# Sample tile last, the first FFN product's operands in the gate's room, weight sums in two sets of tiles: a hybrid S5 and attention layer on one core

## The chip, the cores and the metric

The kernel runs on one core of a Trainium2 chip. Its time is what the device takes for one execution, in microseconds (us); lower is better. A core has five engines with instruction streams of their own: TensorE (PE, matrix products, with a weight load PEld before each), VectorE (DVE), ScalarE (ACT), GpSimd (POOL) and SyncE (SP), which here issues all DMA transfers. An engine works through its stream in order; between engines, semaphores say when an operand is ready.

## What is computed

One layer over 2048 prompt frames and 32 sample frames of width 1024, all in float32. Cut to what matters here:

```python
h = rmsnorm(x, ln1_g) * (1 + sc1) + sh1                 # sc, sh, g1, g2 from c @ w_ada
q, k, v, u = split(h @ w_in)                            # 8 heads, 2 kv heads, 512 state space columns
attn = window_attention(rope(norm(q)), rope(norm(k)), v)   # own chunk of 64 and 128 frames before
y, state = s5(u)                                        # per 16 channels a 64-dim complex scan
g = gelu(y);  ssm_o = g * sigmoid(g @ ssm_glu_w + ssm_glu_b)
x = x + g1 * (concat(rmsnorm(attn), rmsnorm(ssm_o)) @ w_out)
h2 = rmsnorm(x, ln2_g) * (1 + sc2) + sh2
y = x + g2 * ((silu(h2 @ w_gate) * (h2 @ w_up)) @ w_down)   # D_FF = 2816
```

The sample frames take the same layer with a key cache and a state that is handed in. The kernel also returns the last keys, values and states.

## The kernel before

**Precision.** Each float32 operand of a large product is split into a rounded high part and the rest (`split`: a copy on ACT, a subtraction on DVE), and `mm3` makes three matmuls of it: high by high, high by low, low by high.

**Tiles and stages.** The prompt is 16 tiles of 128 frames, the sample is a 17th (number `NPT` = 16) of 32 frames. Stage A makes the projections; stage B runs the state space groups (`ssm_group`, 32 of them) beside attention; stage C (from about 556 to 1011 us) forms the gate of the state space group and the output projection; then comes the FFN.

**Order in stage C.** `TILES` lists the tiles in the order in which attention and the output work on them: the sample, then 8 to 15, then 0 to 7 (tiles 0 to 5 are projected late). `UNITS` lists the gate's units, a unit being two tiles: 8 (the sample alone), then 4 to 7, 0 to 3. Four generators are stepped in turn by the `while` loop at line 1537, through the class `Flow`, one live item each (attention: two):

- `fa`, `attention_tile`: at most `NATT` = 6 tiles ahead of the finished outputs. A softmax goes from TensorE (`s`) over DVE, ACT (`pbuf`) and POOL (`pbuf`) back to TensorE (`pt`, `ob`).
- `fp`, `c_prep` (line 1285): one gate unit. `g_load` brings the gelu of the state space output in (`gr`; for the sample through the DRAM tensor `gs_d` and a transpose of `gn`), `gh` and `gl` are its parts, products with `glh` and `gll` go to the banks `cb`, a tanh makes `z`, and `mh`, `ml` are the gated value's parts. Its limit is `fc.done() // 2 + 2`.
- `fq`, `c_norm` (line 1332): loads the residual `xc`, splits the attention tile into `ah`, `al` and forms both scales (`rb`, `rso`).
- `fc`, `c_out` (line 1363): 48 matmuls of 512 columns (32 for the sample) in two halves to the banks `co`, the scales, the adaLN gate `g1b` on POOL, the residual, and a store to `x1_d`. It is stepped `CST` = 2 times a round. The sample's operand holds high and low part side by side, and `fold` adds the two row groups.

The text order of the program is not the order on the engines: the tile framework's planner (`schedule_with_timeline_sim=True`) lays each engine's stream out at build time from the order of the text and simulated times, and may move what it holds ready ahead.

**Into the FFN.** When attention is through, `ffn_open` and `h_steps(0)` transform the first six finished prompt tiles into the FFN's input quadrants (`q`, from transposes in `ft`). The FFN (three blocks of frames, each a gate-and-up layer `i = 0` and three down layers) makes each 2 by 2 block product with seven products instead of eight (`PRODUCTS`); `steps` numbers them, seven per unit. `start_unit` loads the weight quarters of a unit (`wr`) and forms two sums on POOL; `prepare(n)` forms step n's left operand (`wh`, `wl`), three steps ahead; `prepare_right(n)` forms the right one (`bh`, `bl`, from the quadrants `q`). Both write tiles of the pool `pv`, which is opened after `cin.close()` has closed all pools of stage C.

**Weight sums.** During the first layer of the first block, `down_sums` forms the sums of the down weights that all three blocks read: 12 groups, for each four quarters loaded into the tiles `acc0` to `acc3`, four additions on POOL (a fifth tile, `acc4`, takes one result `ds`), each followed at once by a store to `sd_d`. It is advanced by one step in each product and by two in every fourth.

Of the kernel before, what the change touches and what calls it, by code (L numbers as in the profile page):

```python
# [51 lines left out]
TILES = [NPT, *range(8, NPT), *range(8)]  # L52
UNITS = [8, 4, 5, 6, 7, 0, 1, 2, 3]
# [20 lines left out]
def hybrid_kernel(  # L74
# [1022 lines left out]
    def attention_tile(j):  # L1097
# [21 lines left out]
        if j < NPT:  # L1119
            vcur = kv_split(kf, vf, kt[:, :, 128:256], n)  # L1120
            if j == 8:
# [134 lines left out]

    def cbank(shape, dt=F32, nm="cb"):
        return cs1.tile(shape, dt, tag="cb", name=nm, bufs=CB)
# [11 lines left out]
    def g_load(b):  # L1270

        g = pc2.tile([128, 4, LC, 64], F32, tag="gr", name="gr", bufs=1)
# [12 lines left out]
    def c_prep(u):  # L1285
# [13 lines left out]
        gh = pc2.tile([128, 4, 256], F32R, tag="gh", name="gh", bufs=1)  # L1299
        gl = pc2.tile([128, 4, 256], F32R, tag="gl", name="gl", bufs=1)  # L1300
# [25 lines left out]
        if u in (8, 5, 7, 1):  # L1326
            g_load({8: 2, 5: 3, 7: 0, 1: 1}[u])
# [35 lines left out]
    def c_out(j):  # L1363
# [13 lines left out]
        for h in range(2):  # L1377
# [28 lines left out]
    fp_ = {}  # L1406

# [106 lines left out]
    def down_sums():  # L1514

        for L in layers[1:4]:
            for u in range(2):
                for m in range(2):
                    r = {t: quarter(L, u, m, t, pv.tile([128, 2 * HW], F32, tag=f"acc{i}", name="dq")[
                        :, 0:L.kt * 128].rearrange("p (k n) -> p k n", n=128)) for i, t in enumerate(WHERE)}  # L1520
                    s1 = pv.tile([128, 2 * HW], F32, tag="acc4", name="ds")[:, 0:L.kt * 128].rearrange(
                        "p (k n) -> p k n", n=128)
                    yield 1
                    for i, (o, x, y, op) in enumerate(((s1, r["21"], r["22"], ADD), (r["21"], r["11"], r["21"], SUB),
                                                       (r["11"], s1, r["11"], SUB), (r["12"], r["12"], r["11"], SUB))):
                        tt(P, o, x, y, op)
                        SP.dma_start(sd_d[(L.i - 1) * 4 + 2 * u + m, (0, 2, 1, 3)[i], :, 0:L.kt * 128],
                                     o.rearrange("p k n -> p (k n)"))
                        yield 1

    cg = wo_steps(range(4, 8), stage, 512)
    fp = Flow(c_prep, 9, 1, 0)
    fq = Flow(c_norm, NT, 1, 0)
    fc = Flow(c_out, NT, 1, 0)
    wn = 0
    hg = [None]
    while True:
        more = fa.step(fc.done() + NATT)
        fp.step(fc.done() // 2 + 2)
        for _ in range(CWS):  # L1540
            wn += 1
            advance(cg)
        fq.step(min(fa.done(), 2 * fp.done() - 1, fc.done() + 2))
        if wn > WN:
            for _ in range(CST):
                more = fc.step(fq.done()) or more
        if fa.next == fa.n and not fa.live:
            if hg[0] is None:
                ffn_open()
                hg[0] = h_steps(0)  # L1550
            elif fc.done() >= 7:
                if (layers[0], 0) not in raw:
                    start_unit(0)
                advance(hg[0])
        if not more:
            break
    if hg[0] is None:
        ffn_open()
        hg[0] = h_steps(0)
    for _ in hg[0]:  # L1560
        pass
    if "x1" in dbg:
        SP.dma_start(dbg["x1"], x1_d)
    cin.close()
    ptop.close()
    if upto == "C":
        return
# [235 lines left out]
```

## Time and profile before

| | us |
|---|---|
| median of 3 runs (2440.96 to 2443.54) | 2442.73 |
| profiled execution, its own time | 2443.45 |
| its span, first to last instruction | 2441.7 |
| TensorE busy in the span | 2236.6 |
| VectorE busy | 1771.0 |
| ScalarE busy | 1259.8 |
| GpSimd busy | 1341.2 |
| last output matmul of stage C ends | 1010.9 |
| first FFN matmul starts | 1017.04 |

The mean granted clock of TensorE over the span is 0.954 of full speed. How to read the views that follow: a row of *stretches* gives the length of a part of the span, then for each engine its busy time there and the number of its instructions, then the clock that was granted to TensorE in it, the share of the DMA engines' time and the rate. A row of *waits* gives who waited, for whom, the total, how often, the longest. A row of the *timeline* gives start, length, engine, line, operation, output and inputs; in brackets the idle time of that engine before it and what ended it. Most lines are those of helpers (L89 is `tt`, L101 `act`, L117 `mm`), so the tile names tell the instructions apart. `SPq` is SP issuing a transfer.

### The profile page before, as it was taken

Reading aid. Unit: us, or ns where it says so; the run is one execution under the profiler, and the core shown is the slowest. Engines: PE = TensorE matmul, PEld = TensorE weight load, DVE = VectorE, ACT = ScalarE, POOL = GpSimd, SP = SyncE. Lnnn points to the kernel's source line nnn. Section 1 sums busy time; section 2 is a strip of 40 time slices with the busy share of each in tenths; the row PEclk is TensorE's granted clock in tenths of the full one; section 3 lists DMA queues with packets and bytes.
Section 4 is the critical chain, followed back from the end, with each engine's and each line's share of the span. In section 5 each row is a group of like instructions: output and inputs, shape, how many; then the busy total and the mean of one; then the engine's idle time right before and its main releaser. Section 6 shows DMA issues by size and latency. Waiting matters only on the chain.

```text
span 2441.7 us, 39053 instructions
## 1 busy us (share of the span) xinstructions
PE 2236.6 (92%) x13262; PEld 2071.0 (85%) x13262; DVE 1771.0 (73%) x2722; ACT 1259.8 (52%) x2547; POOL 1341.2 (55%) x1205
## 2 busy tenths in 40 slices
PE   7888897987987889789999999999999989999998
PEld 4677676776777777689899998999999989999998
DVE  6979865787666654576666888865578887777787
ACT  6655433556555555433444557444456664444664
POOL 1277866782644545688855235655542366565232
PEclk7899998997998898889999999999999999999999
DMA  7757767754222124368743654543346446433653
GB/s 232 263 178 212 224 205 229 240 181 142 68 65 72 48 59 149 118 194 255 213 124 105 185 161 153 184 139 119 101 131 205 136 121 183 144 109 99 201 156 124
DMA packets 429573, 380.13 MB, mean 156 GB/s; under 512 B 57326, under 2 KB 358986, under 8 KB 429372
## 3 DMA queue, kind: packets, MB, share of 16 engines
q1 hardware_dynamic: 429372, 377.63, 50.6%
q8 instruction: 104, 1.70, 0.3%
q14 instruction: 97, 0.79, 0.1%
HBM read 284.63 MB, written 92.91 MB: 155 GB/s over the span
## 4 chain that ended last, share of the span: by engine, by line
PE 47%; DVE 4%; DMA 2%; issue 1%; POOL 1%; ACT 0%; SPq 0%; DVEq 0%; POOLq 0%; ACTq 0%
PE fx L117 27%; PE fy L117 13%; PE fz L117 6%; DVE wl L89 2%; DVE bl L89 1%; DMA wr<-in_w_up_dram 1%; POOL dq L89 1%; DMA dq<-in_w_down_dram 1%; PE fo L1640 0%; DVE q L89 0%; POOL c L89 0%; DMA xf<-x_d 0%; PE ft L1437 0%; POOL wr L89 0%; DVE xr L89 0%
## 5 line engine op out<-in xcount | busy, mean ns | idle before, releaser
L89 DVE TENSOR_TENSOR wl<-wr,wh 128x512 fp32r<-128x512 f32 (+1 forms) x714 | 722.9, 1030 | 241.8 <-ACT wh L101 237.7
L101 ACT ACTIVATE wh<-wr 128x512 fp32r<-128x512 f32 (+1 forms) x714 | 434.1, 616 | 561.5 <-PE fx L117 303.2
L117 PE MATMUL fx<-bh,wh 128*128 128x352 f32 (+1 forms) x1584 | 514.3, 325 | 18.5 <-ACT c L101 8.3
L117 PE MATMUL fx<-bh,wl 128*128 128x352 f32 (+1 forms) x1584 | 513.8, 324 | 5.4 <-DVE wl L89 5.4
L117 PE MATMUL fx<-bl,wh 128*128 128x352 f32 (+1 forms) x1584 | 512.9, 324 | 6.1 <-DVE bl L89 6.1
L89 POOL TENSOR_TENSOR wr<-wr 128x512 f32<-128x512 f32 x264 | 394.3, 1503 | 162.2 <-DVE wl L89 145.3
L117 PEld LDWEIGHTS fx<-bh,wh 128*128 128x128 f32 x1584 | 302.3, 191 | 21.4 <-ACT c L101 9.3
L117 PEld LDWEIGHTS fx<-bl,wh 128*128 128x128 f32 x1584 | 302.9, 191 | 7.1 <-DVE bl L89 7.0
L117 PEld LDWEIGHTS fx<-bh,wl 128*128 128x128 f32 x1584 | 301.8, 191 | 6.1 <-DVE wl L89 6.0
L117 PE MATMUL fy<-bh,wl 128*128 128x352 f32 (+1 forms) x792 | 255.9, 323 | 8.2 <-DVE wl L89 8.2
L117 PE MATMUL fy<-bh,wh 128*128 128x352 f32 (+1 forms) x792 | 255.3, 322 | 2.2 <-DVE acc L98 2.2
L117 PE MATMUL fy<-bl,wh 128*128 128x352 f32 (+1 forms) x792 | 254.8, 322 | 0.0
L89 POOL TENSOR_TENSOR c<-c 128x352 f32<-128x352 f32 (+1 forms) x99 | 146.5, 1481 | 166.2 <-ACT wh L101 107.6
L89 POOL TENSOR_TENSOR c<-c,acc 128x352 f32<-128x352 f32 (+1 forms) x72 | 84.3, 1175 | 173.2 <-ACT c L101 169.7
L117 PEld LDWEIGHTS fy<-bh,wl 128*128 128x128 f32 x792 | 149.9, 189 | 8.7 <-DVE wl L89 8.7
L89 POOL TENSOR_TENSOR q<-q,q 128x1408 f32<-128x1408 f32 (+3 forms) x24 | 87.8, 3661 | 118.9 <-DVE q L89 86.7
L89 DVE TENSOR_TENSOR bl<-q,bh 128x1408 fp32r<-128x1408 f32 (+3 forms) x84 | 148.8, 1773 | 5.6 <-ACT bh L101 5.6
L117 PEld LDWEIGHTS fy<-bh,wh 128*128 128x128 f32 x792 | 150.4, 190 | 2.7 <-DVE acc L98 2.7
L117 PEld LDWEIGHTS fy<-bl,wh 128*128 128x128 f32 x792 | 150.3, 190 | 0.0
L101 ACT ACTIVATE bh<-q 128x1408 fp32r<-128x1408 f32 (+3 forms) x84 | 107.7, 1284 | 51.5 <-DVE q L89 28.2
L117 PE MATMUL fz<-bh,wl 128*128 128x352 f32 (+1 forms) x396 | 129.5, 327 | 2.3 <-DVE wl L89 2.2
L117 PE MATMUL fz<-bh,wh 128*128 128x352 f32 (+1 forms) x396 | 128.6, 325 | 3.1 <-ACT wh L101 3.0
(386 smaller groups left out, 5214.9 us busy)
## 6 DMA issues: line engine op xcount, KB each, us to landing
wr<-in_w_gate_dram SPq DMA_DIRECT2D x132, 256.0 KB
wr<-in_w_up_dram SPq DMA_DIRECT2D x132, 256.0 KB
wr<-sd_d SPq DMA_DIRECT2D x96, 256.0 KB
wr<-in_w_down_dram SPq DMA_DIRECT2D x72, 256.0 KB
adw<-in_w_ada_dram SPq DMA_DIRECT2D x64, 256.0 KB
f_d<-c SPq DMA_DIRECT2D x88, 176.0 KB
sm<-sm_d SPq DMA_DIRECT2D x32, 448.0 KB
q<-f_d SPq DMA_DIRECT2D x16, 704.0 KB
```

The source lines that it names most:

```text
L89: e.tensor_tensor(out, a, b, op=op)
L101: A.activation(out, a, func, **kw)
L117: PE.matmul(out, lhsT, rhs, start=start, stop=stop, skip_group_check=more)
```

## The change

The sample goes to the end of both lists, and what followed from its first place is adapted (which prompt unit loads the next `gr`, the limit of `c_norm`, the row at which the earlier keys are loaded). The gate's working tiles get a pool of their own, `pcg`, opened last; once the last gate unit is through, `left_open` closes it and opens the pool `pfv` in its room, which holds the left operands of each fourth step and the right operand `b11` of the first product. `prepare(0)` is called right then, inside the loop. `h_steps(0)` is advanced by two steps a round and from six finished tiles on. `down_sums` works in place in two sets of four tiles, loads a group while the one before is added, and issues each store two additions later; it is advanced by one step in each product, and what is left of it is run at the start of the first down layer.

```diff
-TILES = [NPT, *range(8, NPT), *range(8)]
-UNITS = [8, 4, 5, 6, 7, 0, 1, 2, 3]
+TILES = [*range(8, NPT), *range(8), NPT]
+UNITS = [4, 5, 6, 7, 0, 1, 2, 3, 8]
...
+    pcg_ = ExitStack()
+    pcg = pcg_.enter_context(tc.tile_pool(name="pcg", bufs=1, reuse_waits="tile"))
...
-        g = pc2.tile([128, 4, LC, 64], F32, tag="gr", name="gr", bufs=1)
+        g = pcg.tile([128, 4, LC, 64], F32, tag="gr", name="gr")
...
-        gh = pc2.tile([128, 4, 256], F32R, tag="gh", name="gh", bufs=1)
-        gl = pc2.tile([128, 4, 256], F32R, tag="gl", name="gl", bufs=1)
+        gh = pcg.tile([128, 4, 256], F32R, tag="gh", name="gh")
+        gl = pcg.tile([128, 4, 256], F32R, tag="gl", name="gl")
...
-            z = pc2.tile([128, 2, 256], F32, tag="z", name="z")
+            z = pcg.tile([128, 2, 256], F32, tag="z", name="z", bufs=2)
...
-        if u in (8, 5, 7, 1):
-            g_load({8: 2, 5: 3, 7: 0, 1: 1}[u])
+        if h:
+            g_load({2: 3, 3: 0, 0: 1, 1: 4}[b])
...
-                ta, to = (pc2.tile([128, 512], F32, tag="z", name="fo")[0:n] for _ in range(2))
+                fo = pc2.tile([128, 4, 256], F32, tag="sq", name="fo", bufs=1)[0:n].rearrange("p (a k) n -> p a (k n)", a=2)
+                ta, to = fo[:, 0], fo[:, 1]
...
+    def left_open():
+
+        pcg_.close()
+        fp_["v"] = ctx.enter_context(tc.tile_pool(name="pfv", bufs=1, reuse_waits="tile", side="right"))
...
-            h, l = (pv.tile([128, 4, 128], F32R, tag="wv", name=nm, bufs=4 * AHEAD + 4)[:, 0:L.kt] for nm in ("wh", "wl"))
+            h, l = ((pv if n % 4 else fp_["v"]).tile([128, 4, 128], F32R, tag="wv", name=nm, bufs=12 if n % 4 else 4)[
+                :, 0:L.kt] for nm in ("wh", "wl"))
...
-            h, l = (pv.tile([128, 4, HW], F32R, tag=f"b{t}{bn}", name=f"b{t}")[:, 0:L.kt, 0:w] for t in "hl")
+            h, l = ((fp_["v"] if i == 0 else pv).tile([128, 4, HW], F32R, tag=f"b{t}{bn}", name=f"b{t}")[
+                :, 0:L.kt, 0:w] for t in "hl")
...
+    def down_sums():
+
+        groups = [(L, u, m) for L in layers[1:4] for u in range(2) for m in range(2)]
+        got = {}
+
+        def load(i):
+            if i < len(groups):
+                L, u, m = groups[i]
+                got[i] = {t: quarter(L, u, m, t, pv.tile([128, 2 * HW], F32, tag=f"acc{4 * (i % 2) + k}", name="dq")[
+                    :, 0:L.kt * 128].rearrange("p (k n) -> p k n", n=128)) for k, t in enumerate(WHERE)}
+
+        def store(o):
+            L, u, m, s, x = o
+            SP.dma_start(sd_d[(L.i - 1) * 4 + 2 * u + m, s, :, 0:L.kt * 128], x.rearrange("p k n -> p (k n)"))
+
+        load(0)
+        out = []
+        for i, (L, u, m) in enumerate(groups):
+            yield 1
+            r = got.pop(i)
+            for s, o, x, y, op in ((0, "22", "21", "22", ADD), (2, "21", "11", "21", SUB), (1, "11", "22", "11", SUB),
+                                   (3, "12", "12", "11", SUB)):
+                tt(P, r[o], r[x], r[y], op)
+                out.append((L, u, m, s, r[o]))
+                if len(out) > 2:
+                    store(out.pop(0))
+                if s == 2:
+                    load(i + 1)
+                yield 1
+        for o in out:
+            store(o)
...
-        fq.step(min(fa.done(), 2 * fp.done() - 1, fc.done() + 2))
+        fq.step(min(fa.done(), 2 * fp.done(), fc.done() + 2))
...
-            elif fc.done() >= 7:
+            elif fc.done() >= 6:
                 if (layers[0], 0) not in raw:
                     start_unit(0)
-                advance(hg[0])
+                advance(hg[0], 2)
+                if fp.next == fp.n and not fp.live and "v" not in fp_:
+                    left_open()
+                    prepare(0)
...
     for n in range(6):
-        prepare_right(n)
-        if n < AHEAD:
+        if (layers[0], n) not in right:
+            prepare_right(n)
+        if n < AHEAD and n not in left:
             prepare(n)
...
         if li == 0 and u:
-            advance(sums, 1 + (n % 4 == 0))
+            advance(sums)
+        elif li == 1 and (u, p) == (0, 0):
+            for _ in sums:
+                pass
```

More of the change, by code (lines that the diff above doesn't have):

```diff
@@ L1120, in attention_tile @@
             vcur = kv_split(kf, vf, kt[:, :, 128:256], n)
-            if j == 8:
+            if j == TILES[0]:
                 pkv = pb2.tile([128, 2, 128], F32, tag="ckv", name="pkv", bufs=1)
@@ L1512, in load_left @@
                 raw[n, m] = x
[L1514 to L1542, printed above, removed]
-        fq.step(min(fa.done(), 2 * fp.done() - 1, fc.done() + 2))
[L1544 to L1550, printed above, removed]
-            elif fc.done() >= 7:
-                if (layers[0], 0) not in raw:
-                    start_unit(0)
-                advance(hg[0])
-        if not more:
-            break
@@ L1557, in hybrid_kernel @@
[L1557 to L1567, printed above, removed]
-    pv = ctx.enter_context(tc.tile_pool(name="pv", bufs=1, reuse_waits="tile"))
-    pwr = ctx.enter_context(tc.tile_pool(name="pwr", bufs=1, reuse_waits="tile", side="right"))
-    fs1 = ctx.enter_context(tc.tile_pool(name="fs1", bufs=1, space=bass.MemoryType.PSUM, reuse_waits="tile", side="right"))
@@ new lines, in hybrid_kernel @@
+    cg = wo_steps(range(4, 8), stage, 512)
+    fp = Flow(c_prep, 9, 1, 0)
+    fq = Flow(c_norm, NT, 1, 0)
+    fc = Flow(c_out, NT, 1, 0)
+    wn = 0
+    hg = [None]
+    while True:
+        more = fa.step(fc.done() + NATT)
+        fp.step(fc.done() // 2 + 2)
+        for _ in range(CWS):
+            wn += 1
+            advance(cg)
+        fq.step(min(fa.done(), 2 * fp.done(), fc.done() + 2))
+        if wn > WN:
+            for _ in range(CST):
+                more = fc.step(fq.done()) or more
+        if fa.next == fa.n and not fa.live:
+            if hg[0] is None:
+                ffn_open()
+                hg[0] = h_steps(0)
+            elif fc.done() >= 6:
+                if (layers[0], 0) not in raw:
+                    start_unit(0)
+                advance(hg[0], 2)
+                if fp.next == fp.n and not fp.live and "v" not in fp_:
+                    left_open()
+                    prepare(0)
+        if not more:
+            break
@@ new lines, in hybrid_kernel @@
+    if hg[0] is None:
+        ffn_open()
+        hg[0] = h_steps(0)
+    for _ in hg[0]:
+        pass
+    if "v" not in fp_:
+        left_open()
+    if "x1" in dbg:
+        SP.dma_start(dbg["x1"], x1_d)
+    cin.close()
+    ptop.close()
+    if upto == "C":
+        return
+    pv = ctx.enter_context(tc.tile_pool(name="pv", bufs=1, reuse_waits="tile"))
+    pwr = ctx.enter_context(tc.tile_pool(name="pwr", bufs=1, reuse_waits="tile", side="right"))
+    fs1 = ctx.enter_context(tc.tile_pool(name="fs1", bufs=1, space=bass.MemoryType.PSUM, reuse_waits="tile", side="right"))
@@ L1728, in hybrid_kernel @@
         if li == 0 and u:
[L1729 removed]
+            advance(sums)
+        elif li == 1 and (u, p) == (0, 0):
+            for _ in sums:
+                pass
         load_left(n + FAR)
```

## The prediction

> **What bounds the kernel now.** I read the page, then the busy time by stretches of the span, then TensorE's waits where it is not busy, and last the rows around the stage borders.
>
> ```profile
> PE   7888897987987889789999999999999989999998
> ...
> PEclk7899998997998898889999999999999999999999
> ```
>
> From the middle on, the FFN, TensorE is full at full clock; the first half is not. The change touches the second part of that half, the output stage (from 556 us), and the head of the FFN (1011 to 1221 us). By stretches (columns: length, busy time and instructions of PE, weight loads, DVE, ACT, POOL, then granted clock, DMA share, GB/s):
>
> ```profile
> 556.00:620.00 64.00, 46.28 (x265) 39.02 (x265) 50.60 (x96) 40.09 (x99) 17.14 (x16) 0.79 0.40 119
> 620.00:1011.00 391.00, 339.80 (x1962) 296.18 (x1960) 221.85 (x390) 196.18 (x516) 204.27 (x188) 0.91 0.25 80
> 1011.00:1060.00 49.00, 25.00 (x90) 22.73 (x91) 44.41 (x28) 20.88 (x29) 41.00 (x21) 0.69 0.50 151
> 1060.00:1127.00 67.00, 67.00 (x418) 66.91 (x417) 45.61 (x48) 27.89 (x55) 59.66 (x41) 1.00 0.77 238
> 1127.00:1221.00 94.00, 84.50 (x506) 82.33 (x505) 58.58 (x65) 37.62 (x76) 82.36 (x61) 0.98 0.73 222
> 1221.00:1330.00 109.00, 109.00 (x682) 109.00 (x681) 71.10 (x89) 50.89 (x99) 64.83 (x47) 1.00 0.37 110
> ```
>
> TensorE is the engine that the others must feed in every row but one: in 1011 to 1060 DVE is busy 44.41 of 49. The last row gives TensorE's pace, 109.00/682 = 0.160 us a matmul. By it the 90 matmuls of 1011 to 1060 are 14.4 us of work, so **34.6 us** are lost there, and in 1127 to 1221 506 matmuls are 81.0 us, so **13** are lost. In the output stage 64 - 46.28 = 17.7 us and 391 - 339.80 = 51.2 us are idle, beside time at a lower clock. TensorE's longest wait in the steady part (from 620; total, times, longest):
>
> ```profile
> PE pt L1069 <- POOL pbuf L89: 25.5, 5, 8.2
> ```
>
> and at the start (556 to 620):
>
> ```profile
> PE cb L1281 <- DMA gn<-gs_d: 7.1, 1, 7.1
> ```
>
> Half of the steady idle time is waits on a softmax. The long ones come at a rhythm. The busy time of the instructions on the output banks `co` alone, in three stretches:
>
> ```profile
> 692.00:727.00 35.00, 21.33 (x84) 14.75 (x82) 2.24 (x3) 2.03 (x3) 1.00 0.21 72
> 678.00:688.00 10.00, 0.00 (x0) 0.00 (x0) 0.58 (x1) 0.72 (x1) 0.68 0.20 51
> 735.00:745.00 10.00, 0.00 (x0) 0.00 (x0) 0.66 (x1) 0.69 (x1) 0.56 0.00 0
> ```
>
> and of all instructions, in two:
>
> ```profile
> 692.00:727.00 35.00, 34.81 (x222) 30.62 (x220) 20.08 (x37) 18.25 (x52) 16.72 (x17) 1.00 0.21 72
> 678.00:692.00 14.00, 6.07 (x23) 5.21 (x22) 10.67 (x20) 7.35 (x26) 8.38 (x8) 0.63 0.14 37
> ```
>
> Where output matmuls run, TensorE has no gap (34.81 of 35), attention's chains included. Where none runs, at 678 and again at 735, it idles and then runs at half clock. So the stage has a hole in its supply of output matmuls every other tile.
>
> **The change, part by part.** The sum is made against the profiled execution's 2443.45 us (its span is 2441.7; the median of the runs shown, 2442.73, is 0.7 less).
>
> *A, start of the output stage.* The sample tile leaves the front. With it go the round trip through `gs_d` (7.1 us, above) and the need for the gate's prompt operands to come second; its matmuls move to the end. In their place the first prompt unit's load is now what starts the stage:
>
> ```profile
> 588.12 3.03 SPq L1275 DMA_DIRECT2D gr<-gt_d  x4
> 592.85 1.11 ACT L101 ACTIVATE gh<-gr 128x512 fp32r<-128x512 f32 x1 [4.47 <-DMA gr<-gt_d]
> ```
>
> Today it is issued at 588, and ACT has it 4.7 us later. Moved to about 558 it stands on SP's queue before the `w_out` loads and behind the last `gt_d` store, and its 4.7 us lie beside the attention tiles that are in flight, where today's 7.1 did not since the transposes of `gn` stood before those tiles in TensorE's order. I take a gain of 7. From below, the load could hold up SP and the first gate for twice its 4.7 us (-9); from above, all of the 17.7 us idle could go and the loss by the clock (at 0.79 some 27 of the 64 us are at half, at least 9 of them busy, so 5 to 13 lost): 31. Attention's first six tiles are worked ahead of this stage, and one of them is now a prompt tile in place of the sample: the same matmuls, moved to a stretch where the page has 7 to 9 tenths; I cost it at nothing, since what it adds there it saves here.
>
> *B, steady part.* This term comes from the loop, not from an edited instruction. A gate unit takes eight rounds (seven yields), a `c_norm` four, a `c_out` five (nine yields, two calls a round). Unit u may start at `fc.done() >= 2u-2`. Today position 0 is the sample, so unit u holds positions 2u-1 and 2u, and 2u-2 done means that the *first* tile of unit u-1 has just ended. Seven rounds of gate and three of norm follow before the next output can start, and the second tile of unit u-1 covers five: 15 rounds for two tiles, five without output. That is the hole seen above. After the change unit u holds positions 2u and 2u+1, and the same condition means that unit u-2 has ended; the ten rounds of gate and norm lie exactly beside the ten of unit u-1's two outputs. `2*fp.done()` in place of `2*fp.done()-1` says the same. So the hole closes, with the same matmuls.
>
> Its price comes from the hole at 678: 14 - 6.07 = 7.9 us idle; at 0.63 some 10.4 of the 14 us are at half clock, 2.4 to 6.1 of them busy, which loses 1.2 to 3 more. So about 10 a hole. Seven pairs of tiles (391 us at some 55) follow one another here, and the last two have no attention left to wait for; five such holes make 50; the waits themselves are covered rather than gone, and where the planner's guess of a softmax is short TensorE will still stand, so I keep a quarter back and take **38**. Bounds: 0, if the holes stay, and 65, all of 51.2 and 2 us of clock for each of seven pairs. DVE (222 of 391 busy) and ACT (196) have room for a shorter stage. `h_steps`, which forms the FFN's input, must still be through by its end, in 40 rounds fewer:
>
> ```profile
> L101 ACT ACTIVATE q<-ft,sh,sc x24: 368/615/697, 938.8 to 982.9; 128x352 f32<-128x352 f32 x8, 128x32 f32<-128x32 f32 x8, 128x320 f32<-128x320 f32 x8
> ```
>
> Today it ends 28 us ahead of the last output (about 1011). It now goes two steps a round, 11 rounds for its 22, from six finished tiles on: the output matmuls still cover it, at nothing; uncovered its 24 evictions would be 15 us.
>
> *C, border to the FFN.* The timeline of the border, for ACT, SP's queue and TensorE:
>
> ```profile
> 1014.48 0.63 ACT L101 ACTIVATE t<-xc 128x512 f32<-128x512 f32 x1 [4.75 <-POOL xc L89]
> 1015.02 0.19 ACT L101 ACTIVATION_READ_ACCUMULATOR t<-xc 128x1 f32 x1
> 1015.11 1.36 ACT L101 ACTIVATE bh<-q 128x1408 fp32r<-128x1408 f32 x1
> ```
>
> ```profile
> 1014.89 2.14 SPq L1482 DMA_DIRECT2D dq<-in_w_down_dram  x4
> ```
>
> ```profile
> 1017.04 0.66 PE L117 MATMUL fx<-bh,wh 128*128 128x352 f32 x1 [6.13 <-ACT wh L101]
> ```
>
> Nothing that writes the FFN pool `pv` is issued on an engine before that engine's last instruction of the output stage: ACT had been idle for 4.75 us, its operand `q` was complete (row above), and still `bh` follows `t<-xc`. I read this as the planner's order at the pool's opening. The change frees the room of the gate's working tiles early (`pcg`) and puts the first product's weights and `b11` there, so ACT's three splits, DVE's `bl`, two `wl` and `b12 - b11`, and POOL's `b22 - b12` and four `wr` differences no longer stand behind the border. What such instructions cost there (groups by form, 1011 to 1060; busy us, mean ns), and `wl` later on (1221 to 1330):
>
> ```profile
> L89 DVE TENSOR_TENSOR wl<-wr,wh 128x512 fp32r<-128x512 f32 x15 | 22.2, 1518 | 0.0
> L89 DVE TENSOR_TENSOR bl<-q,bh 128x1408 fp32r<-128x1408 f32 x7 | 18.5, 2658 | 1.1 <-ACT bh L101 1.1
> L89 DVE TENSOR_TENSOR q<-q,q 128x1408 f32<-128x1408 f32 x2 | 4.3, 2162 | 0.0
> ```
>
> ```profile
> L89 POOL TENSOR_TENSOR wr<-wr 128x512 f32<-128x512 f32 x8 | 18.2, 2284 | 4.4 <-DVE wl L89 4.4
> ```
>
> ```profile
> L89 DVE TENSOR_TENSOR wl<-wr,wh 128x512 fp32r<-128x512 f32 x58 | 58.8, 1024 | 26.3 <-ACT wh L101 26.2
> ```
>
> DVE, without a gap here, sets the first unit's pace. It loses 2.66 + 2.16 + 2 x 1.52 = **7.9 us** of work. Nothing else is taken from the chain: the second product still waits for the border, and it then becomes what is late, 24 matmuls or 3.8 us after the first. The sample tile as the last one lengthens the tail before the border:
>
> ```profile
> L128 DVE COPY fo<-co x4: 682/682/682, 600.7 to 615.5; 32x512 f32<-32x512 f32 x4
> L89 DVE TENSOR_TENSOR fo<-fo,co x4: 669/676/676, 602.5 to 618.7; 32x512 f32<-32x512 f32 x4
> ```
>
> ```profile
> 607.70 1.70 POOL L89 TENSOR_TENSOR t<-t,g1b 32x512 f32<-32x512 f32 x1 [0.75 <-DVE t L98]
> ```
>
> One fold stands behind its last matmul, 0.68 + 0.68, and a 32-row step of POOL is no shorter than a whole one; I charge the fold and half such a step, 2.2. New on SP's queue is the reload of `g1b` for 32 rows, which waits for POOL's last use by tile 7; behind it stand tile 7's stores, and nothing on TensorE's path reads those. Last, `wl` takes 1518 ns here against 1024 later, where POOL does less: 13 us of POOL work gone (four `wr`, one `q`) may give back half of that difference over the 13 `wl` left, 3.2. Sum 7.9 - 2.2 + 3.2 = **9**; bounds -3 (only the longer tail) and 22.
> The Trainium skill, SBUF — State Buffer, section "SBUF: two separate sides", says that a DVE instruction with two SBUF inputs and a GpSimd instruction exclude each other and that the loser blocks for the other's whole length. By that rule the 13 us moved would free DVE for up to 13 us and C would be 19, unless the weight sums fill the place at once, when it would be 6. The two `wl` rows agree in sign, at 0.5 us on an average `wl` and not a whole POOL instruction, so 19 (a time of 2371) stays an end of the range; the 6 is R4 below.
>
> *D, weight sums.* The additions on POOL (shortest, median, longest ns):
>
> ```profile
> L89 POOL TENSOR_TENSOR dq<-dq x24: 992/1462/1750, 1028.5 to 1209.4; 128x512 f32<-128x512 f32 x16, 128x384 f32<-128x384 f32 x8
> L89 POOL TENSOR_TENSOR ds<-dq x12: 1007/1468/2660, 1021.4 to 1202.6; 128x512 f32<-128x512 f32 x8, 128x384 f32<-128x384 f32 x4
> ```
>
> POOL's other work from 1014 to 1215:
>
> ```profile
> L89 POOL TENSOR_TENSOR wr<-wr 128x512 f32<-128x512 f32 x47 | 76.8, 1648 | 4.4 <-DVE wl L89 4.4
> ```
>
> ```profile
> L89 POOL TENSOR_TENSOR c<-c 128x352 f32<-128x352 f32 x16 | 21.0, 1311 | 0.0
> ```
>
> and who waited from 1000 to 1215, on SP's queue, POOL and ACT:
>
> ```profile
> SPq L1482 <- DMA sd_d<-dq: 17.7, 12, 4.8
> ```
>
> ```profile
> POOL dq L89 <- DMA dq<-in_w_down_dram: 11.5, 4, 6.8
> ```
>
> ```profile
> ACT wh L101 <- POOL wr L89: 28.2, 9, 9.4
> ACT wh L101 <- DMA wr<-in_w_up_dram: 23.6, 8, 6.3
> ```
>
> A unit of seven products is 168 x 0.160 = 27 us of TensorE. POOL owes it 8 `wr` (13.2) and 3 `c` (3.9), 17.1 us. Of 60 sum steps 48 are additions of about 1.47. At 5 steps in 4 products (today) a unit adds 7 of them, 10.3, and POOL needs 27.4 of 27, with its waits more: it is late, `wr` is late, ACT waits for it. At one step a product (after) it adds 5.6, 8.2, and needs 25.3. The same instructions end later, at step 67 of 77. The fifth tile goes, the second set of four lets a group load while the other is added (11.5 us of POOL's waiting), and a store is issued two additions after its own, so that SP less often stands for POOL. Still, a load into a set must wait for that set's stores, and the last of these is issued just ahead of it, so the 17.7 us of SP waiting, with `wr` loads behind, stay in part. Of the 13 us I take **8**; bounds -2 and 13.
>
> **Sum**: 7 + 38 + 9 + 8 = 62; 2443.45 - 62 = 2381.
>
> **The rivals.**
> *R1, the holes stay.* The order of the engines is the planner's and not the loop's; it has shown that it moves work ahead (SP loads `dq` at 1014.89 for a step that is written seven products later). Then B is 0 to 10, and the time about 2443.45 - (7 + 5 + 9 + 8) = 2414. For it: the waits at the holes are attention chains that exist in either order. Against: a planner can only fill with what is ready, and no output is.
> *R2, attention starves (slower).* Output matmuls now always stand between attention's. A tile's chain crosses TensorE some ten times (`qb` twice, `kb`, `s` twice, `pt` three or four times, `ob` twice), and each time 12 output matmuls may stand in front (84 of them take 21.33 us, so 3 us): up to 30 us a tile, 15 with two in flight, 165 over the 11 tiles left. A quarter of that, 41, with B gone and 24 from the rest, is 17 slower: 2460. It decides from 24/11 = 2.2 us a tile on. Against it: 692 to 727 holds both kinds, with no gap.
> *R3, the operands are not early.* `prepare(0)` is called in the loop, `prepare_right(0)` only behind it; if the planner leaves `bh` and `bl` behind the border, C is -2.2 + 3 = 1 and the time 2389.
> *R4, the sums fill the first unit.* With two sets loaded, up to eight additions are ready there in place of today's six; if DVE then gets nothing back, C is 5.7, and if `wr` is late as before, D is 0: 2393.
>
> **How the numbers follow.** Forecast (about 2350 to 2405) 0.55, R1 0.20, R3 0.08, R4 0.07, R2 0.06, and 0.04 that A to D net to nothing. The low end, 2350, is A to D at 15 + 55 + 14 + 10 = 94 saved; the high end, 2424, at 0 + 8 + 5 + 6 = 19, R1 with less from the rest. They leave out R2, the case of nothing and some of the forecast's and R1's edges, two in ten. A measurement of this kernel can tell about 0.2% (4.9 us) from no change: faster 0.55 + 0.20 + 0.08 + 0.07 = 0.90, the same 0.04, slower 0.06.
>
> **What would show it.** A: no `gn` wait near 560, the first 12-matmul group on prompt operands before 600. B: no stretch of 10 us without `co` between the second tile and the last, granted clock near 1.0, the stage some 45 us shorter. C: `fx` within 1 us of the last `co`, a stall at the second product. D: 1.0 clock and no `wr` waits where 1127 to 1221 was. Wrong would make it: the `pt` waits still at a pair's rhythm (R1), `rb` or `al` waiting for attention (R2), `bh` still behind the last `t<-xc` (R3).

## The result, and the profile after

| | before | after |
|---|---|---|
| median, 4 runs each, side by side | 2443.14 (2440.96 to 2448.02) | 2380.72 (2379.13 to 2381.01) |
| ratio, with its 95% interval | | 0.9741 (0.9724 to 0.9757) |
| profiled execution, its span | 2443.45, 2441.7 | 2380.64, 2378.8 |
| mean granted clock | 0.954 | 0.962 |

The time fell by 62.4 us. The page's slices, after (the same two rows as before):

```profile
PE   7898998997999999699999998999999989999998
...
PEclk8898998999899999799999999999999999999999
```

The output stage is slices 10 to 17 in both: 7 9 8 7 8 8 9 7 became 7 9 9 9 9 9 9 6, and the 6 is the border to the FFN. By stretches, after (columns as before; the first row is the whole output stage, the others its parts and the head of the FFN):

```profile
559.00:963.00 404.00, 365.30 (x2172) 315.98 (x2173) 288.05 (x469) 229.52 (x594) 237.43 (x208) 0.93 0.31 97
559.00:620.00 61.00, 47.50 (x261) 39.62 (x262) 49.88 (x80) 40.02 (x90) 24.53 (x18) 0.80 0.48 151
620.00:963.00 343.00, 317.80 (x1912) 276.36 (x1912) 238.16 (x389) 189.50 (x505) 212.89 (x190) 0.95 0.28 88
963.00:1008.00 45.00, 29.48 (x139) 27.54 (x138) 42.00 (x29) 21.57 (x34) 37.14 (x21) 0.80 0.67 201
1008.00:1070.00 62.00, 61.73 (x376) 61.15 (x374) 47.71 (x44) 25.07 (x50) 62.00 (x42) 0.97 0.90 274
1070.00:1159.00 89.00, 83.17 (x497) 82.54 (x498) 66.25 (x67) 38.13 (x76) 81.80 (x59) 0.96 0.68 208
```

The steady part lost 48 us of length (391 to 343). Of the 51.2 us that TensorE stood idle in it, 25.2 are left, and its busy time fell by 22 us with 50 matmuls fewer in the stretch (8 us at its pace), the rest going with the granted clock (0.91 to 0.95). From the stage's end on TensorE does 139 matmuls in 45 us, against 90 in 49 before. TensorE's longest waits in the steady part, after:

```profile
PE pt L1069 <- POOL pbuf L89: 10.8, 4, 5.3
PE co L117 <- DVE fo L89: 3.7, 1, 3.7
PE pt L1069 <- DVE st L89: 3.7, 1, 3.7
```

The wait on a softmax is 10.8 us where it was 25.5. The second row is new: it lies in the sample tile's tail.

To place every gain, the span of each kernel is cut at five points of the timeline: start of the first `co` matmul, end of the last, start of the FFN matmuls that open its 8th, 43rd and 78th product (24 matmuls to a product). The column "to the 8th product" is the border and the FFN's first unit of seven products together; the next two are 35 products each. Lengths in us:

| | first `co` at | stage: `co` to `co` | to the 8th product | to the 43rd | to the 78th | rest |
|---|---|---|---|---|---|---|
| before | 573.1 | 437.9 | 61.9 | 147.9 | 135.4 | 1085.5 |
| after | 572.5 | 389.6 | 52.5 | 144.5 | 134.9 | 1084.8 |
| order alone | 573.7 | 385.7 | 63.8 | 146.3 | 135.5 | 1087.7 |
| hole closed, sample first | 576.9 | 393.8 | 65.5 | 146.3 | 135.9 | 1086.2 |
| hole back, sample last | 576.6 | 453.4 | 50.0 | 145.7 | 134.9 | 1085.2 |
| gate one tile further ahead | 572.9 | 401.5 | 51.9 | 144.4 | 134.9 | 1085.6 |
| pool opened late | 570.5 | 391.8 | 51.0 | 146.3 | 134.9 | 1084.8 |
| operands in the big pool | 569.7 | 383.0 | 68.0 | 143.4 | 135.4 | 1089.1 |
| `b22 - b12` written later | 570.1 | 391.6 | 51.5 | 144.5 | 135.0 | 1084.1 |
| old sums | 570.2 | 391.8 | 49.0 | 144.8 | 135.0 | 1083.7 |
| sums written later | 569.9 | 391.8 | 51.5 | 146.7 | 135.0 | 1084.4 |
| one set of sum tiles | 571.5 | 388.8 | 48.8 | 152.9 | 134.9 | 1085.4 |
| sums gated | 569.2 | 391.2 | 44.5 | 138.8 | 141.4 | 1085.4 |
| gated, stores later | 573.2 | 391.2 | 44.3 | 140.5 | 140.3 | 1084.4 |

Each row is one profiled execution. The row "`b22 - b12` written later" turned out to have the changed kernel's own instruction order on all five engines, so it is a second measurement of the same program: its parts agree with those of after within 2.4 us, and its median, from another set of runs, is 2383.43 (ratio 0.9742, 0.9728 to 0.9755). Differences of 2 us in a part are therefore not read.

From before to after: stage -48.3, border with the first unit -9.4, the next 35 products -3.4, all else -1.8.

### The profile page after: what moved, and what is told of

Same layout as the page of the kernel before. It is cut to its first block, busy times and chain, and to the rows that moved or that the text cites. A ratio compares the mean times of both kernels' runs of the same rounds, so it can differ in the third digit from the quotient of the medians.

```text
span 2378.8 us, 39058 instructions
## 1 busy us (share of the span) xinstructions
PE 2221.1 (93%) x13262; PEld 2058.2 (87%) x13262; DVE 1802.9 (76%) x2722; ACT 1259.6 (53%) x2549; POOL 1349.8 (57%) x1205
## 3 DMA queue, kind: packets, MB, share of 16 engines
q1 hardware_dynamic: 429372, 377.63, 51.9%
## 5 line engine op out<-in xcount | busy, mean ns | idle before, releaser
L89 DVE TENSOR_TENSOR wl<-wr,wh 128x512 fp32r<-128x512 f32 (+1 forms) x714 | 736.0, 1048 | 220.4 <-ACT wh L101 217.5
L89 POOL TENSOR_TENSOR c<-c 128x352 f32<-128x352 f32 (+1 forms) x99 | 146.7, 1482 | 173.1 <-ACT wh L101 107.9
```

Of the source, the lines that this page charges most:

```text
L89: e.tensor_tensor(out, a, b, op=op)
```

## The experiments

Times are medians; the ratio is to the kernel before, run beside each.

| | us | ratio (95%) |
|---|---|---|
| order alone | 2390.83 | 0.9771 (0.9740 to 0.9803) |
| hole closed, sample first | 2406.35 | 0.9833 (0.9815 to 0.9852) |
| hole back, sample last | 2443.15 | 0.9990 (0.9979 to 1.0000) |
| gate one tile further ahead | 2391.98 | 0.9779 (0.9765 to 0.9792) |
| pool opened late | 2383.23 | 0.9745 (0.9730 to 0.9760) |
| operands in the big pool | 2395.91 | 0.9796 (0.9778 to 0.9814) |
| `b22 - b12` written later | 2383.43 | 0.9742 (0.9728 to 0.9755) |
| old sums | 2376.36 | 0.9718 (0.9705 to 0.9731) |
| sums written later | 2382.26 | 0.9739 (0.9725 to 0.9752) |
| one set of sum tiles | 2384.14 | 0.9752 (0.9738 to 0.9767) |
| sums gated | 2370.85 | 0.9693 (0.9680 to 0.9706) |
| gated, stores later | 2376.20 | 0.9712 (0.9698 to 0.9726) |

### The order and the hole

**Order alone**, on the kernel before:

```diff
-TILES = [NPT, *range(8, NPT), *range(8)]
-UNITS = [8, 4, 5, 6, 7, 0, 1, 2, 3]
+TILES = [*range(8, NPT), *range(8), NPT]
+UNITS = [4, 5, 6, 7, 0, 1, 2, 3, 8]
...
-        fq.step(min(fa.done(), 2 * fp.done() - 1, fc.done() + 2))
+        fq.step(min(fa.done(), 2 * fp.done(), fc.done() + 2))
...
```

> The kernel before with the order alone changed (sample tile last, units renumbered, the loads of the residual halves and the two limits that belong to them); no early operands, old weight sums. My theory, steps A and B: 45 us less than before at the output stage, less the longer tail of 2.2, so 2443 - 43 = 2400, and 2390 to 2403 if the 48 us that the changed kernel's trace shows between the stage's start and its end are all due to the order. Rival 1, part of the stage's gain is owed to the early operands or the freed room (the planner orders around them): 2405 to 2425. Rival 2, the longer tail with the border unprepared costs more than 2.2, since the second set of operands now waits for a later end: 2403 to 2408.

Measured 2390.83, stage 385.7: 52.2 us shorter than before, border and head of the FFN unchanged within 2 us. So the order gives most of the whole gain with nothing else changed, and more than predicted.

**Hole closed, sample first**: one number of the kernel before.

```diff
-        fp.step(fc.done() // 2 + 2)
+        fp.step((fc.done() + 1) // 2 + 2)
```

> The kernel before, sample tile still first, with one number changed: a gate unit may start one finished tile earlier, so that its ten rounds of gate and norm lie beside two output tiles as they do in the changed kernel. My theory (the hole is the loop's 15 rounds for a pair, step B): 38 us less, 2405, with 2395 to 2410 as its range. Rival 1 (the holes are waits on attention's chains, and the sample tile at the front is what makes them): within 5 us of before, 2438 to 2448. Rival 2 (the earlier gate takes TensorE's and ACT's time from attention, whose softmax then is late): slower, 2450 or more.

Measured 2406.35. Counted from the generators' yields, the loop of before makes 134 rounds of which 38 in eight holes have no live output; this one makes 99 with one hole of three; the changed kernel 96 with none. The output stage in the kernel before, then in this one, by stretches:

```profile
556.00:1011.00 455.00, 386.08 (x2225) 335.20 (x2224) 272.45 (x484) 236.27 (x614) 221.40 (x204) 0.89 0.28 85
```

```profile
556.00:971.00 415.00, 371.49 (x2224) 324.60 (x2223) 282.02 (x486) 229.42 (x611) 228.14 (x204) 0.93 0.30 91
```

The same matmuls, but for one record, in 40 us less: 25.4 us of it idle time (68.9 to 43.5), 14.6 us busy time, which goes with the granted clock (0.89 to 0.93). Rival 1 falls, since the sample tile is still first, and rival 2 too.

**Hole back, sample last**: the changed kernel with that number the other way.

```diff
-        fp.step(fc.done() // 2 + 2)
+        fp.step((fc.done() + 1) // 2 + 1)
```

> The changed kernel, sample tile last, with one number changed: a gate unit may start one finished tile later, which brings the five rounds without output back. My theory: 38 us lost, 2381 + 38 = 2419, and 2410 to 2429 as its range. Rival (the sample tile's place made the gain, not the rounds): 2381 to 2386.

Measured 2443.15: 62.4 us lost against the changed kernel, more than expected, all of the change's gain. The loop makes 136 rounds, 40 of them in eight holes. Its output stage:

```profile
559.00:1030.00 471.00, 389.34 (x2196) 332.73 (x2195) 270.91 (x469) 235.06 (x604) 229.60 (x210) 0.88 0.27 84
```

Against the changed kernel's 404 us: 43.0 more idle, and 24.0 more busy, of which 24 more matmuls in the stretch are some 4; the rest goes with the lower clock (0.88 against 0.93). That the hole makes the loss is shown; the size is not additive. Eight holes cost 63.8 us of stage here (8 each), seven cost 44.1 with the sample first (6.3 each). What makes a hole dearer with the sample last is open.

**Gate one tile further ahead**: the edit of the second experiment on the changed kernel.

> The changed kernel with a gate unit allowed one finished tile earlier still, so that gate and norm stand a tile ahead of the output. My theory: the hole is closed already, the loop gains no round, 2378 to 2384. Rival 1 (the pt waits left, 3.7 to 5.3 us at 690, 737 and 836, are want of ready output work): up to 10 less, 2371. Rival 2 (attention starves: gate work one tile earlier stands in front of its chains): over 2390.

Measured 2391.98, 11 slower, stage 401.5 against 389.6. The loop has the same 96 rounds and no hole. TensorE's waits in the steady part:

```profile
PE rb L117 <- DVE sa L1354: 10.8, 5, 3.4
PE co L117 <- ACT t L101: 7.0, 4, 3.3
PE pt L1069 <- POOL pbuf L89: 2.9, 2, 2.6
```

The softmax waits nearly go, and five waits of the norm (`rb`, for the row sums `sa`) and four of the output's own evictions come in their place. Rival 2 is right by its number; its mechanism only in part, since attention ends no more than 5 us later (898 against 893).

### The first product's operands

**Pool opened late**: the early call goes, and `pfv` is opened behind the output stage.

```diff
-                if fp.next == fp.n and not fp.live and "v" not in fp_:
-                    left_open()
-                    prepare(0)
...
-    if "v" not in fp_:
-        left_open()
...
+    pcg_.close()
     cin.close()
     ptop.close()
+    fp_["v"] = ctx.enter_context(tc.tile_pool(name="pfv", bufs=1, reuse_waits="tile", side="right"))
```

> The changed kernel with the FFN's pool opened behind the output stage again, so that no operand of the first product is formed before it. My theory, step C: the 7.9 us of DVE work and the 3.2 of relief come back, 2381 + 11 = 2392; if also the 3.7 us that TensorE waited in the sample tile's tail (a column instruction of DVE took 2.34 us beside a long one of POOL) go with the early work, 2388. Rival 1 (the second product waits for the border anyhow, so the early operands buy nothing): 2381 to 2383. Rival 2 (the rule by which a DVE instruction stands still for the whole of POOL's: the Trainium skill, SBUF — State Buffer, section 'SBUF: two separate sides'; 13 us of POOL work moved): 2381 + 21 = 2402.

Measured 2383.23, as if the call didn't matter, and so it is. ACT's timeline in this kernel:

```profile
942.34 1.37 ACT L101 ACTIVATE bh<-q 128x1408 fp32r<-128x1408 f32 x1
...
967.33 0.63 ACT L101 ACTIVATE t<-xc 32x512 f32<-32x512 f32 x1 [0.86 <-POOL xc L89]
```

`bh` is formed 25 us ahead of the stage's last instruction although its pool is opened behind it in the text. The experiment did not take away what it was meant to; it shows that the planner moves the operands ahead wherever the call stands. That their room decides is shown by the next run.

**Operands in the big pool**: the same, with those tiles in `pv`, whose room is that of the closed stage.

```diff
-            h, l = ((pv if n % 4 else fp_["v"]).tile([128, 4, 128], F32R, tag="wv", name=nm, bufs=12 if n % 4 else 4)[
+            h, l = ((pv if n % 4 else fp_["v"]).tile([128, 4, 128], F32R, tag="wv", name=nm, bufs=16)[
...
+    fp_["v"] = pv
```

> The changed kernel with the first product's weights and its right-hand operand back in the FFN's big pool, so that their room is that of the closed stage as before; order and weight sums as changed. The run with the separate pool opened late showed the operands formed early all the same, so this asks whether the room decides. My theory now (room, not the place of the call): bh, wl and bl are issued behind the stage's last output, the FFN's lag at its seventh product rises from 24.5 to some 32, and the time is 2381 + 10 = 2391, less 3.7 if the slow column instruction in the sample tile's tail goes with the early work: 2387 to 2391. Rival (the early operands buy nothing, since the second product waits for the border either way): 2379 to 2383 with the operands late.

Measured 2395.91, and the operands are late. ACT's and TensorE's timeline there:

```profile
960.99 0.18 ACT L101 ACTIVATION_READ_ACCUMULATOR t<-xc 32x1 f32 x1
961.08 1.36 ACT L101 ACTIVATE bh<-q 128x1408 fp32r<-128x1408 f32 x1
```

```profile
963.01 0.66 PE L117 MATMUL fx<-bh,wh 128*128 128x352 f32 x1 [6.14 <-ACT wh L101]
```

Against the changed kernel, border and first unit are 15.5 us longer (68.0 against 52.5) and the stage is 6.6 shorter (383.0 against 389.6). The other pair that differs in the operands (and in the pace of `h_steps`), order alone and old sums, says the same: 14.8 longer, 6.1 shorter. So the early operands gain 15 at the border and take 6 from the stage: **9** net by the parts. By the medians it is 15.2 and 14.5, by the profiled executions 10.1 and 18.4; what these have beyond the 9 lies where the kernels run the same code (some 4 us behind the 78th product in both pairs), and its cause is open.

**`b22 - b12` written later.** Most of the 6 us lie in the sample tile's tail. The changed kernel, on DVE, then on POOL, DVE and TensorE:

```profile
947.38 2.70 DVE L89 TENSOR_TENSOR q<-q,q 128x1408 f32<-128x1408 f32 x1
...
954.41 3.14 POOL L89 TENSOR_TENSOR q<-q,q 128x1408 f32<-128x1408 f32 x1
...
955.23 2.34 DVE L89 TENSOR_TENSOR rso<-rso 128x1 f32<-128x1 f32 x1 [1.64 <-ACT t L101]
957.60 0.68 DVE L89 TENSOR_TENSOR fo<-fo,co 32x512 f32<-32x512 f32 x1
...
958.42 0.66 PE L117 MATMUL co<-woh,mh 128*64 128x512 f32 x1 [3.72 <-DVE fo L89]
958.88 0.63 PE L117 MATMUL co<-wol,mh 128*64 128x512 f32 x1
```

A column instruction of one element a lane takes 2.34 us, ending at 957.57, with POOL's `q` at 957.55; the fold behind it is late, TensorE stands for 3.72 us, and its last eight matmuls start 0.43 us apart in place of 0.23.

```diff
-            tt(P, b12, b22, b12, SUB)
         elif p == 1:
+            tt(P, b12, b22, b12, SUB)
```

> The changed kernel with POOL's b22 - b12 (3.14 us) written with the second product's operands in place of the first's. Theory (this instruction, moved ahead of the sample tile's tail, made DVE's column product take 2.34 us and the output wait 3.72, then run at half clock): the wait at 955 goes, 2381 - 4 = 2377. Rival 1 (the planner moves it there all the same): 2380 to 2383 with the wait in place. Rival 2 (in the first unit its 3.1 us make wr or the third product's operands late): 2382 to 2386.

Rival 1: no engine's order changed. So this run does not remove the wait, but others lack it. From the first start to the last end the sample tile's 32 `co` matmuls take 14.1 us in the changed kernel and 12.4 to 14.0 in the seven other runs that have the wait. They take 8.3 with the operands in the big pool, 8.6 in order alone, and 8.3 with the gate one tile further ahead, where the operands are early too but POOL's long `q` (966.47 to 969.71) stands beside no column. So the price is 4 to 6 us. The long column makes some 2.2 of the 3.72 (2.34 less the usual 0.15). The rest came earlier: the column had to wait 1.64 us for ACT's `t`, whose chain began 2.0 us late, behind DVE's own early `q` (the first line shown).

### The weight sums

**Old sums**: `down_sums` and its rate as before, all else as changed.

```diff
-            advance(sums)
+            advance(sums, 1 + (n % 4 == 0))
...
```

> The changed kernel with the weight sums of before: five tiles, four of them shared by all groups, a store right behind each addition, five steps in four products. Step D as predicted: 8 us lost, 2389. Step D as the two traces' lag between the seventh and the 42nd product shows it (12.5 against 9.1): 3.4 lost, 2384. Rival (the two sets only moved the additions into the first unit, where they cost what they give later): 2379 to 2383, with a shorter first unit and a longer stretch around 1150.

Measured 2376.36, 4 to 7 us faster than the changed kernel's two medians (the intervals of the ratios just overlap): step D's sign was wrong. The parts show where: 2.5 to 3.5 us at the border and first unit (51.5 and 52.5 in the two measurements, against 49.0), none later (144.5 and 144.8). In the FFN's first 45 us six additions start on POOL here, nine in the changed kernel. From the stage's start to the end of the span the parts differ by 2 us only; the rest of the medians' difference is not placed. With late operands the same swap gives 2390.83 against 2395.91, where the intervals overlap.

**Sums written later**: the first step one unit later in the text.

```diff
-        if li == 0 and u:
+        if li == 0 and u > 1:
```

> The changed kernel with the weight sums' steps written one unit of seven products later. Theory (in the first unit POOL's additions make DVE's wl longer, 1488 ns against 1024 later, and DVE sets that unit's pace): the first unit is relieved by a part of the 16 x 0.46 = 7.4 us, 2374 to 2379, the lag at the seventh product under 22. Rival 1 (the planner fetches the sums forward anyhow): 2380 to 2383 and the additions still before the eighth product. Rival 2 (the additions, pressed into fewer units, make wr late there): 2383 to 2388.

Measured 2382.26: rival 1. The additions stand where they stood, and by tiles and shapes the order is the same on all five engines but for two neighbouring loads of SP (at 1063.5 us). The place in the text does not decide.

**One set**: the new sums with four tiles.

```diff
-                got[i] = {t: quarter(L, u, m, t, pv.tile([128, 2 * HW], F32, tag=f"acc{4 * (i % 2) + k}", name="dq")[
+                got[i] = {t: quarter(L, u, m, t, pv.tile([128, 2 * HW], F32, tag=f"acc{k}", name="dq")[
```

> The changed kernel with its weight sums in one set of four tiles; the order of the additions, the stores two additions late and the rate of one step a product stay. Theory (the second set is room, and the planner fills it with additions fetched into the first unit, nine there against six with the old sums, in front of wr): with one set six or fewer stand there, the 2.0 us stall at 1005 goes, 2375 to 2378, as with the old sums (2376). Rival 1 (the late stores or the new rate cost the time, not the room): 2380 to 2383. Rival 2 (step D as predicted, a load must wait for its set's stores and POOL for the load): 2384 to 2389.

Measured 2384.14, against the theory, but its parts split it. The first unit is short, as with the old sums (48.8 against 52.5), and the next 35 products are long (152.9 against 144.5). Waits from the eighth product on, in this kernel, then in the changed one:

```profile
ACT wh L101 <- DMA wr<-in_w_up_dram: 28.2, 7, 8.8
...
POOL dq L89 <- DMA dq<-in_w_down_dram: 10.5, 7, 3.2
```

```profile
ACT wh L101 <- POOL wr L89: 27.9, 10, 6.6
...
ACT wh L101 <- DMA wr<-in_w_up_dram: 9.7, 3, 6.5
```

So the second set does what step D said of it, POOL no longer waits for loads (the changed kernel has no such row), and it is worth 8.4 us there. What D left out is that what else differs from the old sums (no fifth tile, late stores, the rate) costs as much (144.8 with the old sums, 152.9 with the new in one set), and that the room of the second set lets more additions into the first unit (nine in its first 45 us, six with one set), which costs 2.7 to 3.7.

**Sums gated**: each sum tile gets a column from the weight operand prepared last, ahead of its load, so that a group cannot be loaded earlier.

```diff
-                got[i] = {t: quarter(L, u, m, t, pv.tile([128, 2 * HW], F32, tag=f"acc{4 * (i % 2) + k}", name="dq")[
-                    :, 0:L.kt * 128].rearrange("p (k n) -> p k n", n=128)) for k, t in enumerate(WHERE)}
+                got[i] = {}
+                for k, t in enumerate(WHERE):
+                    x = pv.tile([128, 2 * HW], F32, tag=f"acc{4 * (i % 2) + k}", name="dq")
+                    act(x[:, 0:1], f(left[max(left)][0][0][:, 0, 0:1]))
+                    got[i][t] = quarter(L, u, m, t, x[:, 0:L.kt * 128].rearrange("p (k n) -> p k n", n=128))
```

> The changed kernel, two sets, with a column of each sum tile written by ACT, ahead of its load, from the weight operand prepared last, so that no group can be loaded before the FFN is that far (48 column writes of some 0.2 us on ACT). Theory (the additions fetched into the first unit hold up wr and lengthen wl there; spread evenly POOL keeps up): no dq before the eighth product, the lag there under 20, 2368 to 2377. Rival 1 (DVE sets the first unit's pace without POOL): 2376 to 2380. Rival 2 (the additions, moved into later units, make wr late there, or SP's queue stands for the gated loads): 2381 to 2390.

Measured 2370.85 (0.9693, 0.9680 to 0.9706), the fastest of all, and its interval lies below the changed kernel's. By the medians that is 10 us less (13 against the second measurement); from the stage's start to the end of the span the parts give 5.0 (5.4), and where the rest comes from is open. Groups in the FFN's first 45 us, in the changed kernel, then here:

```profile
L89 DVE TENSOR_TENSOR wl<-wr,wh 128x512 fp32r<-128x512 f32 x16 | 23.3, 1488 | 2.1 <-ACT wh L101 2.1
L89 POOL TENSOR_TENSOR dq<-dq 128x512 f32<-128x512 f32 x9 | 18.1, 2025 | 0.0
L89 POOL TENSOR_TENSOR wr<-wr 128x512 f32<-128x512 f32 x6 | 10.9, 1809 | 1.2 <-DVE wl L89 1.2
```

```profile
L89 DVE TENSOR_TENSOR wl<-wr,wh 128x512 fp32r<-128x512 f32 x20 | 20.6, 1063 | 1.9 <-ACT wh L101 1.9
L89 POOL TENSOR_TENSOR wr<-wr 128x512 f32<-128x512 f32 x10 | 18.4, 1860 | 8.8 <-DVE wl L89 8.8
```

Nine additions are gone from the stretch, POOL makes ten `wr` in place of six, and DVE makes 20 `wl` in less time than 16. The first unit is 8.0 us shorter (44.5 against 52.5), the next 35 products 5.7 shorter; 6.5 comes back before the 78th (141.4 against 134.9), where the sums now end. There ACT waits behind a load that SP issued after two stores it had stood for:

```profile
1211.02 1.75 SPq L1591 DMA_DIRECT2D sd_d<-dq  x2
...
1219.02 1.15 ACT L101 ACTIVATE wh<-wr 128x512 fp32r<-128x512 f32 x2 [7.30 <-DMA wr<-in_w_up_dram]
```

**Gated, stores later**:

```diff
-                if len(out) > 2:
+                if len(out) > 3:
                     store(out.pop(0))
-                if s == 2:
+                if s == 1:
                     load(i + 1)
```

> The gated sums again, with each store issued three additions after its own in place of two, and the next group's loads one addition later, so that no store of a set stands behind its reload. In the gated run TensorE waited 3.26 us at 1217 for wh, behind a wr load that SP issued after two stores it had stood for, and the lag grew by 6 us there. Theory (SP's stand for the stores delays wr): that stall goes, 2371 - 6 = 2365, at least under 2368. Rival 1 (POOL's additions, not the stores, are late there): 2369 to 2373. Rival 2 (loads one addition later make POOL wait for dq, 17.3 us already): 2373 to 2380.

Measured 2376.20. The stall at 1217 is gone and one of 2.94 us stands at 1168; from the eighth to the 78th product it takes 280.8 us against 280.2. So a delayed store does not remove the loss but moves it. The profiled executions differ by 3.4 us, and that lies ahead of the stage (first `co` at 573.2 against 569.2), in code that is the same in both; why is open.

## Why the prediction was right or wrong

The forecast, 2381, was right (2380.72), but not by all of its terms: A, B, C and D were 7, 38, 9 and 8; the runs show about 10, 41, 9 and a loss of some 3. These leave 5 of the 62 us unplaced, not far above what two measurements of one program differ by. So that the sum came within 1 us is luck: D missed by some 11, and what A and B gave beyond their terms, with the unplaced 5, made up for it.

**A, the start.** Mechanism right, size low by some 3 if all that the two runs differ by is counted to it. From "hole closed, sample first" to "order alone" stage and border shorten by 9.8 us, the medians differ by 15.5 (the ratios, taken with their intervals, by 15 plus or minus 9). In the former TensorE still waits 8.6 us for `gn` at 562, and one hole of three rounds stands behind the sample tile, which A did not count; at the 6.3 us that five rounds cost, an estimate for it is 3.8 of the 9.8, and what is left is close to A's 7. The load of `gr` and the prompt tile worked ahead cost nothing that can be read: the first `co` starts at 572.5, before 573.1.

**B, the steady part.** Right by mechanism and size: 38 forecast, 44.1 less stage and 40.5 with the border in the run that changes the limit alone. The working had two errors that offset each other: five holes at 10 each with a quarter held back, where the run has seven at 6.3. The hole priced was one of the longest, and the clock was undervalued in it: 14.6 of the 40 us are busy time at the lower clock, more than a third, where the working had 1.2 to 3 in 10. Over half of the idle time that remains in the steady part is softmax waits (14.5 of 25.2 us), as said. The sign that B gave is not fully met: two stretches of 11 and 13 us without an output matmul remain (from 736 and 835 us), and the clock is 0.95. R1 falls with the run that changes the limit alone.

**`h_steps`** was covered within 1.3 us: its last transposes end at 963.35 and the first product starts at 963.00. But the cover is the sample tile's slow tail: with the operands in the big pool the last `co` ends at 952.7 and the transposes 4.2 us behind it.

**C, the border.** The sum, 9, is what the parts show; its terms are not, so the agreement is luck. The operands gain 15 and not 11.1, perhaps because each operand formed early frees POOL and ACT in the first unit as well as DVE; no run separates that. The tail costs 6 more, where only 2.2 for the fold was charged: `b22 - b12` on POOL and `b12 - b11` on DVE were counted as work that stands in front of nothing, and they delay a column and an eviction of DVE that the last output needs (4 to 6 us by the sample tile's matmuls). The reading on which C rested, that nothing of the FFN's pool is issued ahead of an engine's last instruction of the stage, "the planner's order at the pool's opening", was wrong in its reason: the pool's opening does not matter, the room does. R3 falls with it. The stall at the second product came as said (3.98 us at 967, for `wh`, then 4.93 for `wl`).

The rule of the Trainium skill that was weighed there (SBUF — State Buffer, section "SBUF: two separate sides"), that of a DVE instruction with two SBUF inputs and a GpSimd instruction the one that starts first blocks the other for its whole length, is borne out by the column of 2.34 us, which ends with POOL's instruction. By it C was to be 19, or 6 if the sums fill the place at once. They did fill it: with the additions held back the first unit gives another 8.0.

**D, the weight sums.** Wrong in sign, at its lower bound of -2 by the parts and below it by the medians. The step that failed is "at one step a product (after) it adds 5.6, 8.2, and needs 25.3": it took the rate written in the text for the rate on POOL. The planner fetches additions ahead as far as tiles and loads allow; in the first 45 us nine stand there, though the text's first comes with the eighth product. That is R4, which was given 0.07 and a price of 12; it decided D, which lost some 3 against the old sums where 8 were to be gained. The second half of D, fewer waits of POOL and fewer late `wr` loads, is right and is worth 8.4 (ACT's waits for those loads went from 23.6 to 9.7 us), but the old fifth tile with its early stores had been worth as much, and ACT's waits for POOL's `wr`, which D's rate was to shorten, stayed (28.2 before, 27.9 after). With additions held back by a data dependency the first unit and the next 35 products show the pace that D had in view (44.5 and 138.8).

**R2** did not come with this change, since the gate stays level with the output; one tile more of lead costs 11 us, by waits of the norm and the evictions more than of attention.

## What to carry to other kernels

Count a pipeline's rounds from its generators before looking at waits: a limit that is off by one tile made 38 of 134 rounds without output here, and changing that one number alone gave 39 us where the whole change gave 62. Price such a hole as idle time and slow clock together. Where a planner lays out the streams, moving a step in the text moved next to nothing in three runs here; room that is free and data that are ready decided, so that an extra buffer can cost time, by letting work forward into the stretch that has none to spare, and a cheap dependency can give it back.

## What the runs showed of the hardware that was not expected

A column instruction of DVE with two operands in SBUF took 2.34 to 2.36 us in eight runs, and each time it ended within 0.02 us of the POOL instruction of 3.14 to 3.16 us that had started 0.82 us before it. It is not alone: of the 16 such columns of the changed kernel eight began with POOL idle or nearly done and took 0.15 to 0.16 us, and the other eight, of 0.31 to 2.34 us, each ended within 0.02 us of a POOL instruction that had started before them. It goes the other way too: after the change a `wl` that began at 942.45, 0.16 us ahead of a POOL step, kept its 0.68 us, and the step took 1.68 where it takes 1.30. The mean of `wl` over the FFN's first 45 us follows POOL's load: 1.06 us with POOL busy for 27.6 of them (sums gated), 1.49 with 37.1 (after), 1.64 with 40.3 (operands in the big pool).
